# The rows of the first attention's input moved from 1536 to 1088 bytes apart, and the weight buffers from byte 64 to byte 192 of 512

## The chip, the cores and the metric

The kernel runs on one core of a Trainium2 chip. The time is device time in microseconds of one whole execution, from first to last instruction and what lies around them. The engines are named as in the profile: PE is the matrix engine (PEld its weight load), DVE the vector engine, ACT the scalar engine, POOL GpSimd, SP the queue that starts most transfers.

## The reference, cut to what matters

Two transformer blocks over 256 tokens (and 16 meta tokens) of width 1024, all in float32. The first block is this, where `swa` is a windowed attention with sinks and `diff` a differential attention:

```python
u = rms_norm(h, pre_mix_gain[l])
qa, ka, va, qb, kb, vb, g = jnp.split(u @ w_in[l], SPLITS, axis=-1)
...
merged = g_swa * (o_swa @ w_branch_swa[l]) + g_diff * (o_diff @ w_branch_diff[l])
h = h + rms_norm(merged @ w_out[l], post_mix_gain[l])
u = rms_norm(h, pre_ffn_gain[l])
gate_up = u @ w_ffn_in[l]
f = (jax.nn.silu(gate_up[..., :D_FF]) * gate_up[..., D_FF:]) @ w_ffn_out[l]
h = h + rms_norm(f, post_ffn_gain[l])
```

The second block has a gated delta rule beside a sparse attention, then a cross-attention over 256 memory tokens, then a second feed-forward part of the same size (its inner width is 2816 in both), and a last norm.

## The kernel before

**How a product is made.** Activations lie transposed: 128 partitions by 8 rows (`k`), each row the 256 tokens of 128 channels (272 with the meta tokens). A float32 operand is split into two parts of the reduced type `float32r`: `split` writes the rounded part `h` with ACT (L288, L291) and the rest `l` with DVE (L289, L292). `gemm` (L325) makes one block of 128 output channels from 24 matmuls: for each of 8 rows the weight slice `wh` with the input's `h` and `l`, then for each of 8 rows `wl` with `h`. Each matmul loads its own 128x128 weight slice, which is 512 bytes in a partition, and streams one input row of 256 columns (1024 bytes) or 272 columns (1088 bytes). The load for the next matmul runs while the present one streams, so at any time PE reads one input row and one weight slice. `load_w` makes `wh` (ACT, L309) and `wl` (DVE, L311) from `raw`, a transfer of 512 KB that SP starts; all three have their own buffers of 4096 bytes in a partition.

**Which stages there are.** First attention (14 to about 250 us in the profile): 16 queries and 16 gates (32 `gemm` of 256 columns), 8 value blocks of the differential and 2 of the windowed attention (10 `gemm` of 272 columns), the keys as plain float32 matmuls from `u` (L341), and, woven in between, scores (L539), transposes (L597, L606) and weighted sums (L619, L621). Then branch and output products, the first feed-forward part (`ffn_in`: 44 blocks, then 528 matmuls on `f_h` and `f_l`), the memory's keys and values (L821 to L823), the second block's mixer, the cross-attention, the second feed-forward part (44 blocks), and at the end 330 matmuls on L1650 to L1654 with the roles turned: there the weights `wh`, `wl` stream (512 or 256 columns) and the slices of `f_h`, `f_l` are loaded.

**Where things lie.** What counts here is the place of a buffer within 512 bytes of a partition. Every weight slice begins at byte 64 of 512. The input rows of the stages begin at byte 128 of 512: `AT` holds for each of them an offset in elements that brings them there, in tiles a little larger than the rows. For the first attention `AT["first"]` is 112 and the rows are `3 * P` elements (1536 bytes) apart, so that all eight begin at byte 128; its tiles take 12,736 bytes, and `ul` begins 16 elements further in its tile, which undoes the other remainder of that size. The later `uh`, `ul` of the first feed-forward part come out of the same pool, and there the rows are 1024 bytes apart. `mem_h` and `mem_l` begin at byte 64, as the weights do. In what follows the distance of a matmul is the first byte of the row that it streams, less the first byte of the weight slice that is loaded meanwhile, within 512. It is 64 in the first attention's 42 `gemm`s (768 matmuls of 256 columns and 240 of 272) and in 3600 matmuls behind it (128 `gemm`s of 24, and the 528 on `f_h` and `f_l`), 0 in the memory's 384 matmuls, and 448 (that is, 64 bytes below) in the last 330.

**What sets the order.** The code's order is a proposal: a scheduler with a time model of its own places the instructions on each engine and reuses memory by it, and `tc.keep_in_program_order` pins a few. Where a tile lies and which earlier tile it follows there is therefore part of the schedule. In each feed-forward part three blocks have one more matmul, which adds a product with a slice of zeros (`zero`, L328) after the fourth.

Of the kernel before, what the change touches and what calls it, by code (L numbers as in the profile page):

```python
# [17 lines left out]
F32R = mybir.dt.float32r  # L18
# [7 lines left out]
P = 128  # L26
NT = 256
NM = 16
NK = NT + NM
NP = NT + 32  # L30
D = 1024
KT = D // P
# [181 lines left out]
AT = {'ffn1': 112, 'xatt': 0, 'ffn2': 112, 'mem_h': 112, 'mem_l': 112, 'mix_h': 0, 'mix_l': 0, 'ox_h': 0, 'ox_l': 0, 'f': 0, 'first': 112}  # L214
# [7 lines left out]
def _program(tc, d, out):  # L222
# [4 lines left out]
    def new_pool(stack, name, bufs=1, space=None, side=None):  # L227
        kw = {} if space is None else {"space": space}
        if side is not None:
            kw["side"] = side  # L230
        return stack.enter_context(tc.tile_pool(name=name, bufs=bufs, **kw))

    with ctx:
# [4 lines left out]
        gpool = new_pool(ctx, "gen")  # L238
# [3 lines left out]
        hT = rpool.tile([P, KT, NK], F32, name="hT", tag="resA")  # L242
# [14 lines left out]
        def G(n, j=0):  # L257
            o, w = _GC[n]
            return gcol[:, o + j:o + j + 1]
# [25 lines left out]
        def split(h, l, src, gain=None):  # L285

            if gain is None:
                m = act.activation(h, src, AF.Copy)  # L288
                dve.tensor_tensor(l, src, h.bitcast(F32), OP.subtract)  # L289
            else:  # L290
                m = act.activation(h, src, AF.Copy, scale=gain)  # L291
                dve.scalar_tensor_tensor(l, src, gain, h.bitcast(F32), OP.mult, OP.subtract)  # L292
            return m
# [50 lines left out]
        def gemm_long(src, xs, n, use):  # L344

            ps = None
            for k in range(0, len(xs), KT):
                part = xs[k:k + KT]
                ps = gemm(src[:, k * P:(k + len(part)) * P], part, n, use, first=(k == 0),
                          last=(k + KT >= len(xs)), ps=ps)  # L350

        def rsqrt_of(psum_pool, acc, ones, n, out_t):

            st = psum_pool.tile([P, 512], F32, name="st", tag="o")
            pe.matmul(st[:, :n], ones, acc, start=True, stop=True)
            rsqrt_chain(st[:, :n], n, out_t)
# [42 lines left out]
        def sumsq(k, src, acc, n):  # L399
            if k == 0:  # L400
                act.activation(acc, src, AF.Square)
            else:
                s = gpool.tile([P, NK], F32, name="sq", tag="sq", bufs=2)
                act.activation(s[:, :n], src, AF.Square)
                dve.tensor_tensor(acc, acc, s[:, :n], OP.add)
# [4 lines left out]
        def new_u():  # L410
            uh = gpool.tile([P, KT, NK], F32R, name="uh", tag="uh")
            ul = gpool.tile([P, KT, NK], F32R, name="ul", tag="ul")
            return uh, ul

        def rows_at(t, at):

            return t[:, at:at + KT * NT].rearrange("p (a b) -> p a b", a=KT)

        def new_u_at(at, at_l):
            return [rows_at(gpool.tile([P, KT * NK], F32R, name="u" + e, tag="u" + e), a)  # L420
                    for e, a in (("h", at), ("l", at_l))]

        def parts_at(pool_, name, at_h, at_l):
            return [rows_at(pool_.tile([P, KT * NT + P], F32R, name=name + e), at)
# [10 lines left out]
        apool = new_pool(apx, "a")  # L435

        u = gpool.tile([P, KT, NK], F32, name="u", tag="u")
        uh, ul = ([t[:, at + k * 3 * P:at + k * 3 * P + NK] for k in range(KT)] for t, at in (
            (gpool.tile([P, KT * 3 * P + 112], F32R, name="u" + e, tag="u" + e), AT["first"] + (0, 16)[e == "l"])
            for e in "hl"))  # L440

        st = opool.tile([P, 512], F32, name="st", tag="o")
        for _ in range(WARM):
# [21 lines left out]
        rs = gpool.tile([P, NK], F32, name="rs", tag="rs", bufs=2)  # L465
        rsqrt_chain(st[:, :NK], NK, rs)
        for k in range(KT):
            split(uh[k], ul[k], u[:, k, :])
        us = [(uh[k][:, :NT], ul[k][:, :NT]) for k in range(KT)]
        us_v = [(uh[k], ul[k]) for k in range(KT)]  # L470
        us_k = [u[:, k, :] for k in range(KT)]
        ist.close()

# [31 lines left out]
        at = ExitStack()  # L505
# [264 lines left out]
        first = [None]  # L770
# [80 lines left out]
        rsm = mhp.tile([P, NT], F32, name="rsm")  # L851
        act.activation(rsm, st[:, :NT], AF.Copy)

        def post_norm(src_w, xs, gain, res, res_out, g_next, at=0, at_l=0, whole=False):

            fg = mpool.tile([P, 8, NT], F32, name="fg", tag="fg")
            acc = gpool.tile([P, NK], F32, name="acc", tag="acc", bufs=1)[:, :NT]
            for j in range(8):
                def use(o, j=j):
                    act.activation(fg[:, j, :], o, AF.Copy, scale=G(gain, j))  # L860
                    sumsq(j, o, acc, NT)
                gemm_long(src_w[j], xs, NT, use)
            rr = gpool.tile([P, NK], F32, name="rs", tag="rs", bufs=2)
            rsqrt_of(opool, acc, ones_d, NT, rr[:, :NT])
            if whole:
                u = gpool.tile([P, KT, NK], F32, name="u", tag="uh")
            else:
                uh, ul = new_u_at(at, at_l)
            acc2 = gpool.tile([P, NK], F32, name="acc2", tag="acc2", bufs=1)[:, :NT]
            for j in range(8):  # L870
                dve.tensor_tensor(fg[:, j, :], fg[:, j, :], rr[:, :NT], OP.mult)  # L871
                pool.tensor_tensor(res_out[:, j, :], fg[:, j, :], res[:, j, :NT], OP.add)
                if whole:
                    act.activation(u[:, j, :NT], res_out[:, j, :], AF.Copy, scale=G(g_next, j))
                else:
                    split(uh[:, j, :NT], ul[:, j, :NT], res_out[:, j, :], G(g_next, j))
                sumsq(j, res_out[:, j, :], acc2, NT)
            rs2 = gpool.tile([P, NK], F32, name="rs", tag="rs", bufs=2)
            rsqrt_of(opool, acc2, ones_d, NT, rs2[:, :NT])
            if whole:  # L880
                return [u[:, k, :NT] for k in range(8)], rs2[:, :NT]
            return [(uh[:, k, :NT], ul[:, k, :NT]) for k in range(8)], rs2[:, :NT]

        h1 = rpool.tile([P, KT, NT], F32, name="h1", tag="resB")
        us, rs = post_norm(d["w_out1"], [(m_h[:, k, :], m_l[:, k, :]) for k in range(8)],
                           "post_mix", hT, h1, "pre_ffn", at=AT["ffn1"], at_l=AT["ffn1"] + 16)

        def ffn_in(pool_, src_w, us, rs, f_h, f_l):
            zeros = pool_.tile([96, P], F32R, name="zeros")
            pool.memset(zeros.bitcast(F32), 0.0)  # L890
            for j in range(FT):
# [7 lines left out]
                def use_u(o, sg=sg, j=j):  # L899
# [42 lines left out]

        x1 = rpool.tile([P, KT, NK], F32, name="x1", tag="resA")[:, :, :NT]
        us, rs = post_norm(d["w_fo1"], [(f_h[:, k, :], f_l[:, k, :]) for k in range(FT)],
                           "post_ffn", h1, x1, "g_mix", whole=True)
        fst.close()
# [500 lines left out]
        t = tpool.tile([P, 512], F32, name="t", tag="t")  # L1447
# [26 lines left out]
        t = tpool.tile([P, 512], F32, name="t", tag="t")  # L1474
# [62 lines left out]
        added = []  # L1537

        def residual(src_w, xs, res, res_out, g_next, late=(), more=0, at=0):
            uh, ul = new_u_at(at, at)  # L1540
            acc = gpool.tile([P, NK], F32, name="acc", tag="acc", bufs=1)[:, :NT]
            for j in range(8):
                def use(o, j=j):
                    dve.tensor_tensor(res_out[:, j, :], o, res[:, j, :], OP.add)
                    added.append(split(uh[:, j, :NT], ul[:, j, :NT], res_out[:, j, :], G(g_next, j)))
                    sumsq(j, res_out[:, j, :], acc, NT)
                ps = ppool.tile([P, 512], F32, name="s", tag="s") if 2 <= j < 2 + more else None
                gemm(src_w[j], xs, NT, use, ps=ps, late=late if j < 2 + more else ())
            rs2 = gpool.tile([P, NK], F32, name="rs", tag="rs", bufs=2)
            rsqrt_of(opool, acc, ones_d, NT, rs2[:, :NT])  # L1550
            return [(uh[:, k, :NT], ul[:, k, :NT]) for k in range(8)], rs2[:, :NT]

        x2 = rpool.tile([P, KT, NT], F32, name="x2", tag="resB")
        us, rs = residual(d["w_out2"], [(mix_h[:, k, :], mix_l[:, k, :]) for k in range(8)], x1, x2, "g_xattn", (0,1,2,3), 2, AT["xatt"])
        b2.close()

# [23 lines left out]
        for h in range(4):  # L1580
# [4 lines left out]
            t = tpool.tile([P, 512], F32, name="t", tag="t")  # L1585
            t3 = t.rearrange("p (a b) -> p a b", a=2)
            for qb in range(2):
# [9 lines left out]
                l = xpool.tile([P, 1], F32, name="l1", tag="l1", bufs=4)  # L1597
# [19 lines left out]
            split(ox_h[:, 2 * h:2 * h + 2, :], ox_l[:, 2 * h:2 * h + 2, :], o)  # L1617
        x3 = rpool.tile([P, KT, NK], F32, name="x3", tag="resA")[:, :, :NT]
        us, rs = residual(d["w_xo"], [(ox_h[:, k, :], ox_l[:, k, :]) for k in range(8)], x2, x3, "g_ffn", (4,5,6,7), 2, AT["ffn2"])
        xa.close()  # L1620
        mst.close()
# [8 lines left out]
        for qb in range(2):  # L1630
            for kk_ in range(2):
                t = tpool.tile([P, 512], F32, name="t", tag="t")
# [36 lines left out]
        for qb in range(2):  # L1669
# [13 lines left out]
            a = mpool.tile([P, 1], F32, name="ra", tag="ra", bufs=2)  # L1683
# [32 lines left out]
```

## Time and profile before

| | us |
|---|---|
| median of 3 runs | 1007.73 (1005.29 to 1007.76) |
| the profiled execution, whole | 1007.77 |
| its span, first to last instruction | 1005.9 |
| PE busy in the span | 982.8 |
| DVE, ACT, POOL busy | 685.1, 541.3, 222.8 |

The span leaves out 1.9 us around it. A busy engine is one with an instruction under way; PE's matmuls overlap, so a busy PE may still be slower than it could be, and the measure of its pace is the time from one matmul's start to the next one's. The views used are the page's head, the table by stretches, the chain of work that ended last, and PE's timeline.

### The profile page before, as it was taken

Reading aid. Unit: us, or ns where it says so; the run is one execution under the profiler, and the core shown is the slowest. Engines: PE = TensorE matmul, PEld = TensorE weight load, DVE = VectorE, ACT = ScalarE, POOL = GpSimd, SP = SyncE. Lnnn points to the kernel's source line nnn. Section 1 sums busy time; section 2 is a strip of 40 time slices with the busy share of each in tenths; the row PEclk is TensorE's granted clock in tenths of the full one; section 3 lists DMA queues with packets and bytes.
Section 4 is the critical chain, followed back from the end, with each engine's and each line's share of the span. In section 5 each row is a group of like instructions: output and inputs, shape, how many; then the busy total and the mean of one; then the engine's idle time right before and its main releaser. Section 6 shows DMA issues by size and latency. Waiting matters only on the chain.

```text
span 1005.9 us, 18620 instructions
## 1 busy us (share of the span) xinstructions
PE 982.8 (98%) x7218; PEld 915.2 (91%) x7218; DVE 685.1 (68%) x1466; ACT 541.3 (54%) x1097; POOL 222.8 (22%) x258
## 2 busy tenths in 40 slices
PE   9999999999999999999999899999999999999996
PEld 8888898998988989999999888787799999999885
DVE  6788789788655776656544739967687686566534
ACT  5566657667545755555544444335676554444433
POOL 5534326233230213121100312121021011212002
PEclk9999999999999999999999999999999999999999
DMA  6433333332435465555666232333056155555651
GB/s 238 151 110 104 123 126 106 106 126 87 165 120 194 148 210 199 186 184 187 211 199 195 85 127 84 126 105 105 1 167 203 70 181 185 185 186 189 208 189 64
DMA packets 42023, 149.26 MB, mean 148 GB/s; under 512 B 4728, under 2 KB 5376, under 8 KB 41808
## 3 DMA queue, kind: packets, MB, share of 16 engines
q1 hardware_dynamic: 40896, 145.47, 43.8%
q0 software_dynamic: 608, 2.03, 0.7%
q8 instruction: 56, 0.92, 0.4%
q10 hardware_dynamic: 432, 0.59, 0.2%
q14 instruction: 31, 0.25, 0.1%
HBM read 147.01 MB, written 1.06 MB: 147 GB/s over the span
## 4 chain that ended last, share of the span: by engine, by line
PE 57%; DVE 9%; ACT 2%; issue 1%; ACTq 0%; DVEq 0%
PE mm L325 36%; PE mm L341 4%; PE s L325 2%; PE ac L1653 2%; PE ac L1654 2%; PE ac L1650 2%; DVE wl L311 1%; DVE fg L871 1%; PE mm L1413 1%; PE mm L823 1%; DVE ul L292 1%; PE mm L821 1%; PE mm L822 1%; DVE y L1014 1%; DVE base L1158 0%
## 5 line engine op out<-in xcount | busy, mean ns | idle before, releaser
L311 DVE TENSOR_TENSOR wl<-raw,wh 128x1024 fp32r<-128x1024 f32 (+1 forms) x232 | 285.0, 1229 | 101.1 <-ACT wh L309 94.3
L309 ACT ACTIVATE wh<-raw 128x1024 fp32r<-128x1024 f32 (+1 forms) x232 | 242.8, 1048 | 175.0 <-PE mm L325 100.9
L325 PE MATMUL mm<-uh,wh 128*128 128x256 f32 (+1 forms) x1040 | 257.6, 284 | 0.0
L325 PE MATMUL mm<-ul,wh 128*128 128x256 f32 (+1 forms) x1040 | 255.8, 282 | 0.4 <-DVE ul L292 0.4
L325 PEld LDWEIGHTS mm<-uh,wh 128*128 128x128 f32 x1040 | 195.3, 188 | 2.8 <-ACT wh L309 0.6
L325 PEld LDWEIGHTS mm<-ul,wh 128*128 128x128 f32 x1040 | 195.3, 188 | 1.2 <-DVE ul L292 0.8
L325 PE MATMUL mm<-uh,wl 128*128 128x256 f32 (+1 forms) x1040 | 152.2, 283 | 0.0
L325 PEld LDWEIGHTS mm<-uh,wl 128*128 128x128 f32 x1040 | 134.6, 188 | 0.8
L341 PE MATMUL mm<-u,raw 128*128 128x256 f32 (+1 forms) x464 | 109.3, 386 | 0.0
L897 POOL TENSOR_TENSOR sg<-sg,rs 128x256 f32<-128x256 f32 x44 | 50.7, 1154 | 232.1 <-ACT sg L896 232.1
L341 PEld LDWEIGHTS mm<-u,raw 128*128 128x128 f32 x464 | 85.5, 190 | 14.0 <-issue 0.9
L901 DVE TENSOR_TENSOR ft<-mm,sg 128x256 f32<-128x256 f32 x42 | 17.8, 424 | 50.8 <-PE mm L325 49.6
L325 PE MATMUL mm<-f_h,wh 128*128 128x256 f32 x176 | 42.5, 279 | 0.0
L325 PE MATMUL mm<-f_l,wh 128*128 128x256 f32 x176 | 42.5, 279 | 0.0
L895 DVE TENSOR_TENSOR sg<-mm,rs 128x256 f32<-128x256 f32 x40 | 16.9, 423 | 32.2 <-PE mm L325 32.2
L288 ACT ACTIVATE f_h<-ft 128x256 fp32r<-128x256 f32 x44 | 18.3, 417 | 38.1 <-DVE ft L901 38.1
L1653 PE MATMUL ac<-wh,f_l 128*128 128x512 f32 (+1 forms) x110 | 38.3, 349 | 0.0
L1650 PE MATMUL ac<-wh,f_h 128*128 128x512 f32 (+1 forms) x110 | 38.3, 348 | 0.0
L1654 PE MATMUL ac<-wl,f_h 128*128 128x512 f32 (+1 forms) x110 | 38.0, 349 | 0.0
L896 ACT ACTIVATE sg<-sg 128x256 f32<-128x256 f32 x44 | 18.1, 417 | 33.4 <-DVE sg L895 33.4
L325 PEld LDWEIGHTS mm<-f_l,wh 128*128 128x128 f32 x176 | 33.0, 188 | 0.0
L325 PEld LDWEIGHTS mm<-f_h,wh 128*128 128x128 f32 x176 | 33.0, 188 | 0.0
(545 smaller groups left out, 2104.7 us busy)
## 6 DMA issues: line engine op xcount, KB each, us to landing
raw<-w_gu SPq DMA_DIRECT2D x88, 512.0 KB, 4.1
raw<-w_dn SPq DMA_DIRECT2D x22, 512.0 KB, 4.3
raw<-w_pr SPq DMA_DIRECT2D x20, 512.0 KB, 3.4
raw<-w_gate SPq DMA_DIRECT2D x16, 512.0 KB, 3.5
raw<-w_out SPq DMA_DIRECT2D x16, 512.0 KB, 3.6
raw<-w_fo SPq DMA_DIRECT2D x16, 512.0 KB, 3.5
raw<-w_kb SPq DMA_DIRECT2D x8, 512.0 KB, 3.5
raw<-w_vb SPq DMA_DIRECT2D x8, 512.0 KB, 3.5
```

Source lines behind the costliest of these rows:

```text
L288: m = act.activation(h, src, AF.Copy)
L309: act.activation(h[:, :kt * c], raw[:, :kt * c], AF.Copy)
L311: eng.tensor_tensor(l[:, :kt * c], raw[:, :kt * c], h[:, :kt * c].bitcast(F32), OP.subtract)
L325: pe.matmul(o, w[:, k * P:(k + 1) * P], xs[k][i], start=(first and n_ == 0), stop=(last and n_ == len(steps) - 1))
L341: pe.matmul(o, raw[:, k * P:(k + 1) * P], x, start=(k == 0), stop=(k == len(xs) - 1))
L895: dve.tensor_tensor(sg, o, rs, OP.mult)
L896: act.activation(sg, sg, AF.Silu)
L897: pool.tensor_tensor(sg, sg, rs, OP.mult)
L901: dve.tensor_tensor(t, o, sg, OP.mult)
L1650: m = pe.matmul(o, f_h[:, k, tok], h[:, cols], start=(k == 0), stop=False)
L1653: pe.matmul(o, f_l[:, k, tok], h[:, cols], start=False, stop=False)
L1654: pe.matmul(o, f_h[:, k, tok], l[:, cols], start=False, stop=(k == FT - 1))
```

## The change

The first attention's `uh` and `ul` become plain tiles of 8 rows of 272 elements. Their rows are 1088 bytes apart, so each begins 64 bytes further within 512 than the one before. The two tiles take 8704 bytes each in place of 12,736, so what is allocated above them comes down by 8064 bytes: the buffers `raw`, `wh`, `wl`, and the memory's tiles, now begin at byte 192 of 512. The tiles below stay where they were, and the first feed-forward part's rows still begin at byte 128.

```diff
-        def new_u_at(at, at_l):
-            return [rows_at(gpool.tile([P, KT * NK], F32R, name="u" + e, tag="u" + e), a)
-                    for e, a in (("h", at), ("l", at_l))]
+        def new_u_at(at):
+            return [rows_at(gpool.tile([P, KT * NK], F32R, name="u" + e, tag="u" + e), at) for e in "hl"]
...
-        uh, ul = ([t[:, at + k * 3 * P:at + k * 3 * P + NK] for k in range(KT)] for t, at in (
-            (gpool.tile([P, KT * 3 * P + 112], F32R, name="u" + e, tag="u" + e), AT["first"] + (0, 16)[e == "l"])
-            for e in "hl"))
+        uh, ul = new_u()
...
-            split(uh[k], ul[k], u[:, k, :])
-        us = [(uh[k][:, :NT], ul[k][:, :NT]) for k in range(KT)]
-        us_v = [(uh[k], ul[k]) for k in range(KT)]
+            split(uh[:, k, :], ul[:, k, :], u[:, k, :])
+        us = [(uh[:, k, :NT], ul[:, k, :NT]) for k in range(KT)]
+        us_v = [(uh[:, k, :], ul[:, k, :]) for k in range(KT)]
...
-                           "post_mix", hT, h1, "pre_ffn", at=AT["ffn1"], at_l=AT["ffn1"] + 16)
+                           "post_mix", hT, h1, "pre_ffn", at=AT["ffn1"])
```

`new_u` (L410) makes two tiles `[P, KT, NK]`. After the change the distances are these: in the first attention 0, 64, 128 and so on up to 448 for the rows 0 to 7; 448 for the 3600 matmuls that had 64; 0 for the memory's, as before; 64 for the last 330, which had 448. The slice of zeros lies at distance 384 in the first feed-forward part in both, and at 384 in place of 0 in the second.

No instruction is added or removed, and the order of transfers on SP is the same. The smaller tiles change which buffers follow which in memory, and the scheduler then places some instructions of the first attention otherwise, from about 92 to 200 us of the profile; all later order is the same. (After the change the line numbers from L437 on are 3 less.)

On PE, at about 91.3 us, where the scores of two heads (`kb_h`, `kb_l` against `qh`, `ql`) meet a value block of 272 columns (`uh`, `wl`); before:

```order
L539 MATMUL s<-kb_l,qh 128x272
L539 MATMUL s<-kb_h,qh 128x272
L539 MATMUL s<-kb_h,ql 128x272
L539 MATMUL s<-kb_l,qh 128x272
L325 MATMUL mm<-uh,wl 128x272 x3
L597 MATMUL t<-base,pr_222 32x128
L539 MATMUL s<-kb_h,qh 128x272
L539 MATMUL s<-kb_h,ql 128x272
L539 MATMUL s<-kb_l,qh 128x272
L325 MATMUL mm<-uh,wl 128x272 x2
```

and with the change:

```order
L536 MATMUL s<-kb_l,qh 128x272
L536 MATMUL s<-kb_h,qh 128x272
L536 MATMUL s<-kb_h,ql 128x272
L536 MATMUL s<-kb_l,qh 128x272
L536 MATMUL s<-kb_h,qh 128x272
L536 MATMUL s<-kb_h,ql 128x272
L536 MATMUL s<-kb_l,qh 128x272
L325 MATMUL mm<-uh,wl 128x272 x5
L594 MATMUL t<-base,pr_222 32x128
```

Three scores have moved up to the other four, and the value block's matmuls stand together behind them. Over the whole first attention the 192 score matmuls stand in 56 separate groups before and in 52 with the change.

On POOL, in the middle of the first attention, where the rotation of a query (`ropem`, `rot`, `qraw`) and the norm of a finished head (`ms`, `rr`, `osb`) take turns; before:

```order
L514 TENSOR_TENSOR ropem<-rawq,cqt 128x256
L657 TENSOR_TENSOR ms<-ms,rr 128x256
L515 TENSOR_TENSOR rot<-rot,sqt 128x256
L658 TENSOR_TENSOR ms<-ms,rr 128x256
L516 TENSOR_TENSOR qraw<-ropem,rot 128x256
L659 TENSOR_SCALAR ms<-ms 128x256
L660 TENSOR_TENSOR rr<-rr,ms 128x256
L661 TENSOR_TENSOR osb<-osb,rr 128x256
```

and with the change:

```order
L511 TENSOR_TENSOR ropem<-rawq,cqt 128x256
L512 TENSOR_TENSOR rot<-rot,sqt 128x256
L654 TENSOR_TENSOR ms<-ms,rr 128x256
L513 TENSOR_TENSOR qraw<-ropem,rot 128x256
L655 TENSOR_TENSOR ms<-ms,rr 128x256
L656 TENSOR_SCALAR ms<-ms 128x256
L511 TENSOR_TENSOR ropem<-rawq,cqt 128x256
L657 TENSOR_TENSOR rr<-rr,ms 128x256
```

The query's rotation now goes ahead of the norm's first step, and the next query's first step ahead of the norm's last two.

## Rows read from the trace of the kernel before

**Rows 1.** The page's head: span, and busy time of each engine.
```profile
span 1005.9 us, 18620 instructions
PE 982.8 (98%) x7218; PEld 915.2 (91%) x7218; DVE 685.1 (68%) x1466; ACT 541.3 (54%) x1097; POOL 222.8 (22%) x258
```

**Rows 2.** Stretches: length, then busy us (count) by engine, granted clock, DMA share, GB/s.
```profile
170.00:250.00 80.00, 80.00 (x612) 73.13 (x609) 65.80 (x159) 52.74 (x133) 21.30 (x28) 1.00 0.32 106
401.00:486.00 85.00, 85.00 (x724) 85.00 (x723) 51.88 (x75) 44.45 (x61) 17.77 (x16) 1.00 0.56 185
...
823.00:938.00 115.00, 115.00 (x972) 114.72 (x971) 71.51 (x105) 57.81 (x86) 25.32 (x22) 1.00 0.58 188
```

**Rows 3.** Chain that ended last, 401 to 486 us: start, length, work.
```profile
430.16 55.95 PE mm L325 x475
```

**Rows 4.** PE's timeline in the memory's keys: start, length, instruction.
```profile
344.84 0.28 PE L325 MATMUL mm<-mem_h,wh 128*128 128x256 f32 x1
...
345.92 0.28 PE L325 MATMUL mm<-mem_l,wh 128*128 128x256 f32 x1
```

**Rows 5.** PE's timeline in the second block's output product, distance 64.
```profile
734.29 0.28 PE L325 MATMUL s<-mix_h,wh 128*128 128x256 f32 x1
...
747.89 0.28 PE L325 MATMUL mm<-uh,wh 128*128 128x256 f32 x1
```

**Rows 6.** PE's timeline around the first product with zeros, distance 64.
```profile
376.72 0.28 PE L325 MATMUL mm<-uh,wh 128*128 128x256 f32 x1
...
378.65 0.28 PE L325 MATMUL mm<-ul,wh 128*128 128x256 f32 x1
378.77 0.28 PE L328 MATMUL mm<-ul,zeros 96*128 96x256 f32 x1
...
379.94 0.28 PE L325 MATMUL mm<-ul,wh 128*128 128x256 f32 x1
```

**Rows 7.** PE's timeline in the last 330 matmuls, distance 448.
```profile
944.34 0.28 PE L1654 MATMUL ac<-wl,f_h 128*128 128x256 f32 x1
...
944.79 0.39 PE L1650 MATMUL ac<-wh,f_h 128*128 128x512 f32 x1
...
946.88 0.28 PE L1650 MATMUL ac<-wh,f_h 128*128 128x256 f32 x1
...
947.59 0.39 PE L1650 MATMUL ac<-wh,f_h 128*128 128x512 f32 x1
```

**Rows 8.** PE's timeline where distances differ: cross-attention (128), first attention (0, 448 in turn).
```profile
783.64 0.28 PE L1614 MATMUL o<-ptx_h,vx_h 128*128 128x256 f32 x1
...
785.06 0.28 PE L325 MATMUL mm<-ox_l,wh 128*128 128x256 f32 x1
...
100.40 0.28 PE L619 MATMUL o<-pl,va_h 128*128 128x256 f32 x1
...
100.87 0.28 PE L621 MATMUL o<-pm,vam 96*128 96x256 f32 x1
```

**Rows 9.** PE's timeline in a value block of 272 columns, distance 64.
```profile
47.50 0.29 PE L325 MATMUL mm<-uh,wh 128*128 128x272 f32 x1
...
48.76 0.29 PE L325 MATMUL mm<-uh,wh 128*128 128x272 f32 x1
```

**Rows 10.** PE's timeline at the scores of the first order fence.
```profile
91.33 0.29 PE L539 MATMUL s<-kb_h,ql 64*128 64x272 f32 x1
91.46 0.28 PE L539 MATMUL s<-kb_l,qh 64*128 64x272 f32 x1
91.67 0.65 PE L325 MATMUL mm<-uh,wl 128*128 128x272 f32 x3
...
92.35 0.40 PE L539 MATMUL s<-kb_h,qh 64*128 64x272 f32 x1
92.59 0.28 PE L539 MATMUL s<-kb_h,ql 64*128 64x272 f32 x1
```

**Rows 11.** Groups, 14 to 250 us: count, busy us, mean ns, idle before and its releaser.
```profile
L657 POOL TENSOR_TENSOR ms<-ms,rr 128x256 f32<-128x256 f32 x8 | 7.4, 920 | 34.0 <-ACT rr L656 34.0
```

More of the change, by code (lines that the diff above doesn't have):

```diff
@@ L852, in _program, with post_norm @@
         act.activation(rsm, st[:, :NT], AF.Copy)
-        def post_norm(src_w, xs, gain, res, res_out, g_next, at=0, at_l=0, whole=False):
+        def post_norm(src_w, xs, gain, res, res_out, g_next, at=0, whole=False):
             fg = mpool.tile([P, 8, NT], F32, name="fg", tag="fg")
@@ L867, in post_norm @@
             else:
-                uh, ul = new_u_at(at, at_l)
+                uh, ul = new_u_at(at)
             acc2 = gpool.tile([P, NK], F32, name="acc2", tag="acc2", bufs=1)[:, :NT]
@@ L1539, in residual @@
         def residual(src_w, xs, res, res_out, g_next, late=(), more=0, at=0):
-            uh, ul = new_u_at(at, at)
+            uh, ul = new_u_at(at)
             acc = gpool.tile([P, NK], F32, name="acc", tag="acc", bufs=1)[:, :NT]
```

## The prediction

> **What bounds the kernel now.** I read the page's head first: PE is busy in 982.8 of 1005.9 us, the next engine in 685 [rows 1]. [...]
>
> The pace is not one number. [...] The long chain of the first feed-forward part has 475 matmuls in 55.95 us, 117.8 ns each [rows 3]. The memory's keys take 9 steps from 344.84 to 345.92: 120 ns [rows 4]. The output product of the second block takes 120 steps from 734.29 to 747.89: 113.3 ns [rows 5]. Same shape, same clock, no wait of an engine among them. The stages differ in where the streamed row and the weight slice lie: distance 0 in rows 4, distance 64 in rows 3 and 5. So at 64 there are two paces, 118 and 113, and at 0 there is a third, 120. Which of the two paces a run at 64 has is a matter of how it was entered: the first feed-forward part starts at 113 (17 steps from 376.72 to 378.65, 113.5), and from its first product with zeros, whose own distance is 384, it goes at 118 (10 steps from 378.77 to 379.94, 117) and stays there to the end [rows 6, 3]. A run keeps its pace until something disturbs it.
>
> **The change, part by part.** The sum is made against the profiled execution, 1007.77 whole, which is the median's 1007.73 to four hundredths.
>
> *The first attention's rows.* 768 matmuls of 256 columns and 240 of 272 leave distance 64 for distances that go up by 64 from row to row. The trace has no such sequence in a `gemm`. The nearest rows are products whose distance is other than 64 or changes: the cross-attention's weighted sums at 128 take 12 steps in 1.42 us, 118.3 ns, and the first attention's own weighted sums at 0 and 448 by turns take 4 steps in 0.47 us, 117.5 ns [rows 8]. I take 118.0 against the 117.8 that most of these `gemm`s have now: 1008 x 0.2 ns = +0.2 us. The bounds are the fastest and slowest steady paces anywhere: 768 x (113.3 - 117.8) = -3.5 us and 768 x (120 - 117.8) = +1.7 us. For 272 columns there is one pace to read, 10 steps in 1.26 us, 126 ns [rows 9]; I leave it, with +-3 ns by the same spread: +-0.7 us.
>
> *The other 3600 matmuls* go from 64 to 448, from 64 bytes ahead of the weights to 64 behind. Here the trace does show the new distance: the last 330 matmuls have it. Their runs of 256 columns go at one pace or the other by turns, 4 steps from 944.34 to 944.79 at 112.5 ns, 6 steps from 946.88 to 947.59 at 118 ns [rows 7]. These are the two paces of distance 64, and none of 120. So I take the pace of the long runs as it is, 117.8, and the term as 0. But a run of six says little of one of a thousand, and the term is large: at 113.3 throughout it would be 3600 x -4.5 = -16 us, at 120 throughout 3600 x 2.2 = +8 us. Those are its bounds.
>
> *What goes at 113 now* is 120 steps of rows 5, some 20 of rows 6 and a few dozen after rows 5, say 200. Entered anew at another distance, I let half of them fall to 118: 100 x 4.5 ns = +0.5 us; bounds 0 and +0.9.
>
> *The last 330* go from 448 to 64. Both paces are seen at both distances; 0, with +-330 x 2 ns = +-0.7 us.
>
> *The memory's 384* stay at distance 0, since rows and weights move together: 0.
>
> *The order in the first attention.* A score that stands alone costs more at its ends than inside: from 91.33 to 91.46 it is 0.13 us, but the last of a group takes from 91.46 to 91.67, 0.21, and the first of one from 92.35 to 92.59, 0.24 [rows 10]. One group less saves 0.08 + 0.11 = 0.19 us; there are 56 groups before and 52 after, so -0.8 us. On POOL the rotation of a query now goes ahead of a head's norm. POOL stands idle 34.0 us before the norm's first step, waiting for ACT [rows 11], and PE has no idle time in this stage [rows 2]; what is moved lies in that slack: 0. If the cover were gone, because buffers now follow each other more closely and a matmul waits for one, a POOL step is 0.9 us [rows 11]; I allow three of them, +-2.7 us, for what a new order may lose or win.
>
> *What is released.* PE being the bound, a faster pace would be followed by the weights: in the feed-forward parts DVE, the next engine, is busy 52 of 85 us [rows 2], and could stand 113 ns (82 of 85) without being late.
>
> The sum: 0.2 + 0 + 0.5 + 0 + 0 - 0.8 = -0.1 us. 1007.77 - 0.1 = **1007.7 us**.
>
> [...] The paces of rows 3 and 4 differ by 2.2 ns with nothing but the distance different that I can see. [...]
>
> **The rivals.**
>
> *Faster: the long runs go at 113.* At 448 half of the runs in rows 7 have that pace, while of the two long runs at 64 in rows 3 and 5 only the shorter has it; and the products with zeros are disturbances in which a run may change its pace, at distances that the change alters. In the first feed-forward part with its second product, 1056 + 528 matmuls, it would be 1584 x 4.5 = -7 us; in the second, 1056 x 4.5 = -4.8 us. One of them gives 1001 to 1003, both 996. Against it: at 64 the disturbances led to 118, and a run at 118 was not seen to speed up. Chance 0.27.
>
> *Slower: the long runs go at 120.* Streaming 64 bytes behind the weights may not be the mirror of streaming 64 ahead, and rows 7 are too short to see a slow drift into the state of rows 4. The place is the two feed-forward parts with the 528, 2640 matmuls; the price is 2640 x 2.2 = 5.8 us, or 8 with all 3600: 1013.5 to 1015.7. It decides once the pace there passes 119 ns (2640 x 1.2 = 3.2 us). For it: distance 0, only 64 bytes away, has this state and keeps it. Against it: no run at 448 shows it. Chance 0.14.
>
> *Slower: the first attention's spread rows.* No row shows distances from 192 to 320 in sequence, and each change of distance is a disturbance. At 122 ns, the 1008 matmuls would be 4 us late: 1012. Chance 0.11, and 0.06 more that the new order brings waits of about that size: 1011.
>
> *The place does nothing.* What differs between rows 3, 4 and 5 may be something else in those stages. Then only the order is left, -0.8: 1007. Chance 0.08, within the forecast's.
>
> **How the numbers follow.** About 0.3%, 3 us, is what a measurement of this kernel can tell from no change. The forecast (1004.7 to 1010.7) has 0.42 with the last rival in it. Faster by more than that is 0.27, from the first rival; slower is 0.14 + 0.11 + 0.06 = 0.31. The range reaches down to one and a half of the fast runs' gains, -10.7 us, 997, and up to the slower feed-forward parts and a little of the order, +6.3, 1014; a tenth is left out at each end. The likeliest case's own range is 1004.7 to 1010.7.
>
> **What would show it.** In the changed kernel's timeline: the pace of the long chain after the last product with zeros in either feed-forward part, 117.8 by the forecast, 113.3 or 120 by the rivals; steps of about 118 in the first attention's gates; 120 in the memory's keys; the score groups' ends as in rows 10 but fewer; PE busy 80 of 80 us in 170 to 250. If the feed-forward parts take other than 85.0 and 115.0 us, the forecast is wrong by that much, and the second term is the one that failed; if the first attention ends more than 3 us from where it does now, it is the first or the last.

## The result, and the profile after

The changed kernel takes **991.3 us** (990.05 to 992.7, four executions) against 1007.75 (1005.29 to 1008.94, four): a ratio of 0.984, with a 95% interval of 0.9818 to 0.9863. The forecast was no change, 1007.7, with a range of 997 to 1014. It was wrong: the time fell by 16 us, out of the range. The rival "the long runs go at 113" is what happened. The ratios below are against executions of the kernel before on the same chip, whose median was 1007.0 to 1007.8.

The page's head after answers to [rows 1]: PE's busy time is 15.6 us less, with as many instructions.

```profile
span 988.8 us, 18641 instructions
...
PE 967.2 (98%) x7218; PEld 902.1 (91%) x7218; DVE 686.8 (69%) x1466; ACT 545.3 (55%) x1097; POOL 223.4 (23%) x258
```

Where the 17.1 us of the span went is read from PE's timeline, from the first matmul of a stage to the first of the next (differences are of the unrounded times):

| stage | before, us | after, us | difference |
|---|---|---|---|
| first attention, from 13.6 | 234.7 | 232.7 | -2.0 |
| branch products | 57.8 | 57.5 | -0.3 |
| output product (m) | 26.9 | 25.9 | -0.9 |
| memory's keys | 20.6 | 20.6 | 0.0 |
| first feed-forward part, 44 blocks | 132.6 | 126.8 | **-5.8** |
| its 528 on f_h and f_l, then the second block's mixer | 233.8 | 231.4 | **-2.4** |
| second block's output product (mix) | 28.1 | 28.8 | +0.8 |
| into the cross-attention | 31.8 | 30.9 | -0.9 |
| product on ox | 27.5 | 27.3 | -0.2 |
| second feed-forward part, 44 blocks | 129.3 | 125.2 | **-4.1** |
| last 330 matmuls and the output | 69.5 | 68.2 | -1.3 |

Not all of the -5.8 is pace. In the profiled execution before, the granted clock stood at 0.5 for 3.4 us of that stage, after PE had waited 1.4 us for `ul`; 15 matmuls there took 213 ns a step, which cost 15 x (213 - 118) = 1.4 us. The profiled execution of the changed kernel had the same wait and a clock of 1.00 in that stage. Columns as in [rows 2], before:

```profile
357.60:361.00 3.40, 3.40 (x19) 3.40 (x18) 3.40 (x8) 0.42 (x1) 0.00 (x0) 0.51 0.91 306
```

Two stretches serve for every kernel below, since in all of them they lie inside the long runs of one feed-forward part each: 430.5 to 475.5 us in the first, 881.5 to 919.5 in the second. Columns as in [rows 2]; PE's count is what is read. Some 2.4 of it began before the stretch (a matmul is under way for 0.28 us), so 385 in 45 us is a pace of 117.6 ns, 399 is 113.5, 382 is 118.5, and in 38 us 325 is 117.8, 338 is 113.2, 323 is 118.5. Of the kernel before:

```profile
430.50:475.50 45.00, 45.00 (x385) 45.00 (x384) 27.41 (x41) 23.31 (x33) 9.11 (x8) 1.00 0.56 184
881.50:919.50 38.00, 38.00 (x325) 38.00 (x324) 22.67 (x34) 18.18 (x27) 8.42 (x7) 1.00 0.57 182
```

and of the changed one:

```profile
430.50:475.50 45.00, 45.00 (x399) 45.00 (x399) 28.60 (x42) 24.83 (x34) 9.09 (x8) 1.00 0.59 191
881.50:919.50 38.00, 38.00 (x338) 38.00 (x337) 24.15 (x36) 20.78 (x28) 7.58 (x8) 1.00 0.58 194
```

Same shape, same granted clock, PE without a gap in both, so the time there is the number of matmuls by their pace, and only the pace is another.

How it came to that pace stands in the chain that ended last, second feed-forward part of the changed kernel (start, length, work), which answers to [rows 3]:

```profile
805.24 3.30 PE s L325 x28
808.54 8.95 PE mm L325 x76
817.49 0.12 PE mm L328
817.61 16.34 PE mm L325 x144
833.96 0.12 PE mm L328
834.08 32.66 PE mm L325 x288
866.74 0.12 PE mm L328
866.87 53.97 PE mm L325 x476
```

The first 104 steps go at 117.8 ns (3.30 / 28, 8.95 / 76). Then comes the first product with zeros (L328), and behind it 144 steps take 16.34 us, 113.5 ns, and so to the end (53.97 / 476 = 113.4). It is [rows 6] turned round: there the first product with zeros led from 113.3 to 117.8.

In the first feed-forward part another product stands some 28 matmuls ahead of the first one with zeros: `s<-cc,base` (L935, L932 in the changed kernel), with weights of 32 x 8, two matmuls. The pace changes there too. Before, the 45 steps ahead of it go at 117.6 ns (5.29 / 45), and the 27 from 375.70 to the first product with zeros at 378.77 [rows 6] at 113.7:

```profile
369.52 5.29 PE mm L325 x45
...
375.70 0.28 PE L325 MATMUL mm<-ul,wh 128*128 128x256 f32 x1
```

In the changed kernel the steps ahead go at 113.8 (5.12 / 45), and the 27 from 370.50 to 373.68 at 117.8:

```profile
364.48 5.12 PE mm L325 x45
...
370.50 0.29 PE L325 MATMUL mm<-ul,wh 128*128 128x256 f32 x1
...
373.68 0.28 PE L328 MATMUL mm<-ul,zeros 96*128 96x256 f32 x1
```

So the changed kernel needed its first product with zeros in both parts, to come back to 113.4. That product is at distance 384 in the first part of both kernels; it led down in the one and up in the other, so its own distance does not say which way.

The memory's keys, whose distance stayed 0, stayed at 120 ns, 7 steps from 336.80 to 337.64, as in [rows 4]:

```profile
336.80 0.28 PE L325 MATMUL mm<-mem_h,wh 128*128 128x256 f32 x1
...
337.64 0.28 PE L325 MATMUL mm<-mem_l,wh 128*128 128x256 f32 x1
```

### The profile page after: what moved, and what is told of

The parts are those of the page before. It is cut to its first block, busy times and chain, and to the rows that moved or that the text cites. A ratio compares the mean times of both kernels' runs of the same rounds, so it can differ in the third digit from the quotient of the medians.

```text
span 988.8 us, 18641 instructions
## 1 busy us (share of the span) xinstructions
PE 967.2 (98%) x7218; PEld 902.1 (91%) x7218; DVE 686.8 (69%) x1466; ACT 545.3 (55%) x1097; POOL 223.4 (23%) x258
## 4 chain that ended last, share of the span: by engine, by line
PE 56%; DVE 8%; ACT 2%; issue 1%; DMA 0%; ACTq 0%; DVEq 0%
PE mm L325 36%; PE mm L341 4%; PE s L325 2%; PE ac L1651 2%; PE ac L1650 2%; PE ac L1647 2%; DVE fg L868 1%; DVE wl L311 1%; PE mm L1410 1%; PE mm L820 1%; PE mm L818 1%; PE mm L819 1%; DVE ul L292 1%; DVE y L1011 1%; DMA raw<-w_xq 0%
## 5 line engine op out<-in xcount | busy, mean ns | idle before, releaser
L325 PE MATMUL mm<-uh,wh 128*128 128x256 f32 (+1 forms) x1040 | 253.1, 282 | 0.0
L325 PE MATMUL mm<-ul,wh 128*128 128x256 f32 (+1 forms) x1040 | 251.2, 281 | 0.2 <-DVE ul L292 0.2
L325 PE MATMUL mm<-uh,wl 128*128 128x256 f32 (+1 forms) x1040 | 148.6, 281 | 0.0
L325 PEld LDWEIGHTS mm<-uh,wl 128*128 128x128 f32 x1040 | 131.9, 188 | 0.5 <-issue 0.2
L511 POOL TENSOR_TENSOR ropem<-rawq,cqt 128x256 f32<-128x256 f32 x16 | 18.4, 1152 | 59.9 <-ACT rawq L508 59.8
L341 PE MATMUL mm<-os,raw 128*128 128x256 f32 x128 | 28.2, 380 | 0.0
```

The source lines that it names most:

```text
L325: pe.matmul(o, w[:, k * P:(k + 1) * P], xs[k][i], start=(first and n_ == 0), stop=(last and n_ == len(steps) - 1))
L341: pe.matmul(o, raw[:, k * P:(k + 1) * P], x, start=(k == 0), stop=(k == len(xs) - 1))
L511: pool.tensor_tensor(m[:, :n], raw[:, :n], c, OP.mult)
```

## The experiments

Theory: the distance sets which paces a run can have, and a product with zeros lets it change between them. Rivals: the first attention's new rows or order; the weights' own place.

### The distance alone

Kernel before, rows moved and nothing else; tiles and the order of every engine stay.

```diff
-AT = {'ffn1': 112, 'xatt': 0, 'ffn2': 112, ... 'mix_h': 0, 'mix_l': 0, 'ox_h': 0, 'ox_l': 0, 'f': 0, 'first': 112}
+AT = {'ffn1': 80, 'xatt': 96, 'ffn2': 80, ... 'mix_h': 96, 'mix_l': 96, 'ox_h': 96, 'ox_l': 96, 'f': 0, 'first': 80}
```

> The kernel before with the input rows of nine stages 128 bytes lower and nothing else different: weights at byte 64 as before, rows at byte 0, so distance 448 for the first attention's 1008 matmuls, both feed-forward input parts (2112) and the products on mix and ox and into the cross-attention (576). The first attention's rows stay 1536 bytes apart, and the order of every engine is that of before. The 528 matmuls on f_h and f_l and the 384 on od and m stay at distance 64. Theory (the distance sets the pace): the 2112 + 576 go at about 114.3 ns as in the changed kernel in place of 117.8, 2688 x 3.5 = -9.4 us, and the first attention's 768 x 3.5 = -2.7 us: about 996, the feed-forward stretches at 113 to 114 ns. Rival (it was the new rows or the new order of the first attention): 1007 to 1008, pace 117.8 throughout. Second rival (it is the weights' own place, not the distance): 1007 to 1008 too, but then the run with the rows moved up stays at 991.

Measured: 993.25 us, ratio 0.9868 (0.9832 to 0.9905). Both stretches have the changed kernel's counts, to one:

```profile
430.50:475.50 45.00, 45.00 (x400) 45.00 (x399) 29.08 (x42) 24.39 (x34) 9.47 (x9) 1.00 0.61 194
881.50:919.50 38.00, 38.00 (x338) 38.00 (x337) 24.05 (x36) 19.30 (x28) 8.35 (x7) 1.00 0.62 194
```

So 14 of the 16 us come with the first attention's old layout, the old order and the weights at their old place: the first rival falls, and the second. No product with zeros lifted this kernel: both parts had come to 113.4 ahead of their first one, the first part behind L935 (from 117.8), the second for the 76 steps before it. The first attention's 660 intervals go at 115.8 in place of 117.6, the 272 columns at 123.8 in place of 126.1. The 528 on f_h and f_l, left at 64, went at 117.8 here although the run came to them at 113.3.

The other way round: the changed kernel with rows moved up by as much.

```diff
-AT = {'ffn1': 112, 'xatt': 0, 'ffn2': 112, ... 'mix_h': 0, 'mix_l': 0, 'ox_h': 0, 'ox_l': 0, ...}
+AT = {'ffn1': 16, 'xatt': 32, 'ffn2': 16, ... 'mix_h': 32, 'mix_l': 32, 'ox_h': 32, 'ox_l': 32, ...}
```

> The changed kernel with the input rows of the feed-forward parts, the cross-attention and the products on mix and ox 128 bytes higher: weights at 192 as in the change, rows at 256, so distance 64 again for 2688 matmuls; the first attention as in the change, the same order on every engine. Theory (distance): these go back to 117.8 ns, 2688 x 3.5 = +9.4 us over the change's 991.3: about 1001. Rival (rows or order of the first attention, or the weights' own place): 991.

Measured: 1004.73 us, ratio 0.9978 (0.9962 to 0.9995), 13.4 above the change.

```profile
430.50:475.50 45.00, 45.00 (x384) 45.00 (x384) 27.38 (x40) 23.61 (x32) 9.12 (x8) 1.00 0.61 187
881.50:919.50 38.00, 38.00 (x325) 38.00 (x325) 23.50 (x34) 19.82 (x28) 8.10 (x7) 1.00 0.60 189
```

Back at 117.8. The loss is 4 us above the theory's. Of these 528 x 4.4 = 2.3 us are the 528 on f_h and f_l: still at 448, they kept the 117.8 with which the run came to them, with no product with zeros among them to lift it. What is left of the gain on the kernel before is 2.5 us. In the profiled executions the first attention is 0.5 us shorter than before and the last 330 with the output 0.8; the rest is not placed, since shorter stages differ by up to 2.7 us one way and 2.0 the other.

### The products with zeros

The same edit in the changed kernel and in the one before:

```diff
-                gemm(src_w[2 * j], us, NT, use_g, ps=bank(0), zero=zeros if j in (3, 6, 12) else None)
+                gemm(src_w[2 * j], us, NT, use_g, ps=bank(0), zero=None)
```

> The changed kernel without the six products with a slice of zeros (three in each feed-forward part), which add nothing to the result. In the changed kernel the second feed-forward part goes at 117.8 for 102 steps up to the first of them, and at 113.3 behind it. Theory (a product with zeros is what lets a run change its pace): without them that part stays at 117.8 to its end, 950 x 4.5 = +4.3 us, and the first part, which came to 113.3 before its first one, stays there: 995 to 996. Rival (at this distance a run comes to 113.3 by itself in the end): 990 to 991, six products less.

> The changed kernel without products with zeros once more, letter for letter the third run's. Its executions gave four times 997.7 to 998.3 and, in the profiled one, 1003.9 with the first feed-forward part at 117.8 for 1469 steps. Theory (at this distance both paces hold, and without products with zeros the entry decides for the whole run): a profiled execution near 998 shows the first part at 113.3, 1469 x 4.4 = 6.5 us less, and the second at 117.8 as in the other; one near 1004 shows 117.8 in both. Rival (the 6 us are something else, a wait elsewhere): a profiled execution near 998 shows 117.8 in the first part all the same.

Measured: 998.2 us (five executions, 997.73 to 1003.89), ratio 0.9913; the second time 999.63 (four, 996.83 to 1002.93), ratio 0.9923. The two profiled executions, 1003.89 and 1000.39, both show 117.8 to the end in both parts; the second:

```profile
430.50:475.50 45.00, 45.00 (x385) 45.00 (x384) 27.36 (x41) 23.66 (x32) 9.10 (x8) 1.00 0.59 186
881.50:919.50 38.00, 38.00 (x325) 38.00 (x325) 22.80 (x34) 20.12 (x28) 8.49 (x7) 1.00 0.58 184
```

Six products less, and 9.3 us more than the profiled 991.08 of the changed kernel: at 448 a run does not come to 113.3 by itself in 1465 steps, and the rival falls. Half of the first expectation fell too: it took the changed kernel's first part to be at 113.3 ahead of its first product with zeros, but behind L932 it is at 117.8 there, as the lines above show, and here it stayed so. And the second test did not show what it was made for: the 3.5 us between its two profiled executions are not the first part's pace. They lie in several places, of which one is the output product, where the granted clock was 0.83 in one and 1.00 in the other; just before, PE had waited 1.6 us for `m_h` and `m_l` in the one and 1.8 in the other. The stretch from 311 to 321 us, columns as in [rows 2], in the execution of 1003.89:

```profile
311.00:321.00 10.00, 9.21 (x65) 9.21 (x66) 5.08 (x7) 5.74 (x10) 0.00 (x0) 0.83 0.63 199
```

and in the one of 1000.39, with 85 matmuls for 65:

```profile
311.00:321.00 10.00, 9.72 (x85) 9.72 (x86) 6.13 (x8) 6.78 (x13) 0.00 (x0) 1.00 0.71 216
```

What pace the executions near 997 had is not known.

> The kernel before without the six products with zeros, distance 64 everywhere. There the first feed-forward part began at 113.3 and went over to 117.8 at the first of them. Theory (the product with zeros is the kick, at this distance to the slow side): the first part stays at 113.3 for its 1584 matmuls, 1480 x 4.5 = -6.7 us: 1001; the second, which began at 117.8, stays as it is. Rival (at distance 64 the pace falls back to 117.8 whatever disturbs it): 1007.

Measured: 999.35 us, ratio 0.9917 (0.9891 to 0.9943).

```profile
430.50:475.50 45.00, 45.00 (x399) 45.00 (x399) 29.06 (x43) 24.18 (x34) 9.12 (x8) 1.00 0.64 195
881.50:919.50 38.00, 38.00 (x325) 38.00 (x324) 22.77 (x34) 20.30 (x27) 7.60 (x7) 1.00 0.59 181
```

As the theory has it: at distance 64 too a run can keep 113.3, here for 1462 steps with the 528 on f_h and f_l in it, if nothing throws it out. The second part, which began at 117.8, kept that. In the kernel before, the products with zeros alone cost 8 us, most of it by the pace behind the first of them (some 1440 steps x 4.4 ns = 6.3 us).

Then the products were moved: `j in (10, 14, 18)` in the changed kernel.

> The changed kernel with the three products with zeros of each feed-forward part moved from the blocks 3, 6 and 12 to 10, 14 and 18 of 22. Theory (at 448 such a product lifts a run from 117.8 to 113.3 and nothing else does): the second part goes at 117.8 up to block 10 in place of 3, 336 matmuls later, 336 x 4.4 = +1.5 us, and turns there; the first likewise if it begins at 117.8, another +1.5: 992 to 995. Rival (a run comes to 113.3 by itself after some hundred matmuls): the turn stays near step 100, and the time at 991.

Measured: 994.38 us (992.66 to 994.76), ratio 0.9866. The chain in its second part:

```profile
806.70 3.30 PE s L325 x28
809.99 48.53 PE mm L325 x412
858.52 0.12 PE mm L328
858.64 21.78 PE mm L325 x192
880.42 0.12 PE mm L328
880.55 21.78 PE mm L325 x192
```

Now 440 steps go at 117.8 (48.53 / 412), 336 more than the 104 of the changed kernel, and the turn to 113.4 (21.78 / 192) stands again at the first product with zeros. The first part turned in the same way. This is the plainest proof that the product is what lifts the run there.

The products on all 128 rows, `zeros` made `[P, P]` in the changed kernel:

> The changed kernel with the six products with zeros on all 128 rows in place of 96; the same order on every engine. Theory (one more matmul, which makes the sequence of h and l rows start anew, is what lets the pace change): as the changed kernel, 991, and the second feed-forward part goes from 117.8 to 113.3 at the first of them. Rival (the 96 rows are what does it, a slice of another shape between full ones): as without them, 117.8 to the end in the second part, 996 to 998.

Measured: 997.46 us, ratio 0.9904 (0.9883 to 0.9925), undecided: the second part turned at the first of them, so 96 rows are not needed, but the first part did not turn at any of three. That is one of four from 117.8, against five of six on 96 rows at this distance (runs below included).

```profile
430.50:475.50 45.00, 45.00 (x385) 45.00 (x384) 27.56 (x40) 23.45 (x33) 9.10 (x8) 1.00 0.59 188
881.50:919.50 38.00, 38.00 (x338) 38.00 (x336) 24.23 (x35) 20.68 (x29) 8.00 (x7) 1.00 0.59 194
```

### All eight distances

Kernel before, with `AT` set so that each stage has another distance; tiles and order stay. The three settings are those of the three runs below, in their order.

```diff
+AT = {'ffn1': 0, 'xatt': 48, 'ffn2': 16, ... 'mix_h': 48, 'mix_l': 48, 'ox_h': 48, 'ox_l': 48, 'f': 0, 'first': 96}
...
+AT = {'ffn1': 48, 'xatt': 112, 'ffn2': 64, ... 'mix_h': 112, 'mix_l': 112, 'ox_h': 112, 'ox_l': 112, 'f': 0, 'first': 32}
...
+AT = {'ffn1': 16, 'xatt': 96, 'ffn2': 48, ... 'mix_h': 96, 'mix_l': 96, 'ox_h': 96, 'ox_l': 96, 'f': 0, 'first': 0}
```

> The kernel before with nothing moved but the input rows, by stage: first attention at distance 0, first feed-forward part at 128, second at 192, the 576 products into the cross-attention and on mix and ox at 256; the 528 on f_h and f_l and the 384 on od and m stay at 64. Theory (448, rows just below the weights, is the one place from which the products with zeros lead to 113.3): 117.8 in both feed-forward parts, 120 in the first attention, 768 x 2.2 = +1.7 us: 1008 to 1009. Rival (64 is the one bad place, and 0; any other one is as good as 448): both feed-forward parts at 113.3 behind their first product with zeros, some 950 x 4.5 = -4.3 us each, and the 576 at 113.3, -2.6 us, so 998.

Measured: 1005.4 us, ratio 0.9979 (0.9966 to 0.9993). First part at 128, second at 192, and 15 us of the product on mix at 256:

```profile
430.50:475.50 45.00, 45.00 (x382) 45.00 (x381) 27.20 (x39) 23.34 (x32) 9.07 (x8) 1.00 0.57 183
881.50:919.50 38.00, 38.00 (x338) 38.00 (x337) 23.91 (x36) 19.31 (x28) 8.41 (x7) 1.00 0.60 194
...
734.00:749.00 15.00, 15.00 (x127) 15.00 (x126) 14.02 (x20) 10.92 (x21) 6.33 (x4) 1.00 0.49 157
```

> As the run before it with the places that are left: first attention at distance 256, first feed-forward part at 320, second at 384, the 576 at 0. Theory (448 alone): 117.8 in both feed-forward parts, 120 in the 576, +1.3 us: 1008 to 1009. Rival (only 0 and 64 are bad): both parts at 113.3, -8.6 us, the first attention faster by up to 768 x 2 = -1.5 us, so 998.

Measured: 1008.97 us, ratio 1.0025 (1.0012 to 1.0039). First part at 320, second at 384:

```profile
430.50:475.50 45.00, 45.00 (x385) 45.00 (x384) 27.75 (x40) 23.42 (x33) 9.12 (x8) 1.00 0.59 188
881.50:919.50 38.00, 38.00 (x323) 38.00 (x322) 22.51 (x33) 18.11 (x27) 8.38 (x7) 1.00 0.56 181
```

Theory and rival both fell in the pair. 192 went as fast as 448, against the one; 128, 256, 320 and 384 are not, against the other. 256 behaves as 0 (120 ns: 15 us / 124.6), 320 as 64 (first part: 113.3 for 25 steps, 117.8 from the first product with zeros on), 384 as 128 (steps of 115 to 122 in a pattern of five, 288 of them in 34.17 us: mean 118.7; at 128 the 382 in 45 us are 118.5). That made a new theory, the distance within 256, and a run to test it with the parts exchanged:

> The kernel before with the input rows moved by stage: first attention at distance 128, first feed-forward part at 192, second at 320, the 576 at 448; the 528 and the 384 stay at 64. New theory (what counts is the distance within 256: 0 gives 120 ns, 128 a mixture of 118.7, 64 and 192 have both 113.3 and 117.8, and a product with zeros leads to 117.8 at 64 and to 113.3 at 192): the first part ends at 113.3, also behind a start at 117.8; the second at 117.8, also behind a start at 113.3; the first attention near 118.7. First part 1056 x -4.4 = -4.6 us, the 576 up to -2.5, the first attention +0.7: 1001 to 1004 against 1007. Rival (each part of the model has its own pace, whatever the distance; before, 192 was seen in the second part alone and 320 in the first alone): the first part at 117.8, the second at 113.3.

Measured: 1001.62 us, ratio 0.9945 (0.9928 to 0.9962), inside the theory's 1001 to 1004.

```profile
430.50:475.50 45.00, 45.00 (x399) 45.00 (x398) 29.11 (x42) 24.15 (x33) 9.76 (x9) 1.00 0.61 197
881.50:919.50 38.00, 38.00 (x325) 38.00 (x325) 23.88 (x35) 18.95 (x28) 7.84 (x7) 1.00 0.62 192
```

192 in the first part: 113.5; 320 in the second: 117.8; the first attention at 128: 118.9. The rival falls. At 192 and in this run at 320 the long runs had these paces ahead of their first product with zeros, so a lift was seen at 448 alone, and a fall at 64 and 320.

### Two versions meant to be faster

The kernel before with 128 bytes more in the first `ul` tile, the keys' rows brought to 448, and one product with zeros more in each feed-forward part (left out here: `mem_l`, as `mem_h`, and two offsets that keep the later rows at byte 128):

```diff
-            (gpool.tile([P, KT * 3 * P + 112], F32R, name="u" + e, tag="u" + e), AT["first"] + (0, 16)[e == "l"])
+            (gpool.tile([P, KT * 3 * P + 112 + (0, 32)[e == "l"]], F32R, name="u" + e, tag="u" + e), (96, 112)[e == "l"])
...
-        mem_h = mhp.tile([P, 8, NT], F32R, name="mem_h")
+        mem_h = mhp.tile([P, 8 * NT + P], F32R, name="mem_h")[:, 112:112 + 8 * NT].rearrange("p (a b) -> p a b", a=8)
...
-zero=zeros if j in (3, 6, 12) else None
+zero=zeros if j in (0, 3, 6, 12) else None
```

> The first attention's rows 1536 bytes apart as before, its ul tile 128 bytes longer so that weights lie at byte 192 as in the change, rows at 128: distance 448 in the first attention, both feed-forward parts, on od, m, mix, ox, f, and, with 448 bytes ahead in its tiles, in the memory's keys too; the order of before but for one product with zeros more, in the first block of each feed-forward part. Theory (distance and kick): from the change's 991.3, first attention 768 x -2.4 = -1.8 and 240 x -1.7 = -0.4 us (paces as in the run with the rows moved back), the keys 192 x -6 = -1.2, the second part's first 100 steps -0.4, one product each +0.2: 987 to 988. Rival (short runs take either pace by chance): no better than the change, 990 to 992.

Measured: 992.42 us, ratio 0.9858 (0.9842 to 0.9874): no better than the change. The keys did go at 113.5 behind their first 37 steps and the first attention at 116.4, but that stage still took 1.4 us longer than in the change (234.1 against 232.7), 172 steps of the output product and the keys' first went at 117.8, and the first part stayed there for 170 until its third product with zeros.

So more of them were put in, in the first blocks of each stage (`ZS` is their slice; the branch and output products are left out here):

```diff
+            gemm(d["w_xk"][j], mems, NT, ..., zero=ZS if j in (0, 1) else None)
+            gemm(src_w[j], xs, NT, use, ps=ps, ..., zero=ZS if j in (1, 2, 4) else None)
...
+            zeros = ZS
...
+zero=zeros if j in (1, 2, 3, 6, 12) else None
```

> The kernel with distance 448 everywhere, with more products with zeros: one in the first blocks of the branch product, the output product, the memory's keys, the second block's output product, the cross-attention's output, and five in each feed-forward part (blocks 1, 2, 3, 6, 12). Theory: each of these stages turns to 113.3 early. From that kernel's 992.4: its first part 170 x -4.4 = -0.7 us, the output product 170 x -4.4 = -0.7, branch 45 x -4.4 = -0.2, cross-attention's output 70 x -4.4 = -0.3, some 12 products more +1.4: 991.5 or less, 990 where all of them turn. Rival (short runs do not turn, the products are only a cost): 993.8.

Measured: 995.7 us, ratio 0.9883 (0.9865 to 0.99), 3.3 slower. The output product and the keys went at 113.4, and so did the product on mix, which had that pace without added products too; the product on ox stayed at 117.8. The waits of PE from 330 to 376 us (us in total, times, longest) say what became of it:

```profile
PE s L327 <- ACT wh L311: 3.7, 2, 3.1
PE mm L327 <- DVE wl L313: 1.7, 1, 1.7
PE s L327 <- DVE ul L294: 0.2, 1, 0.2
```

In the kernel without the added products PE waited 1.8 us there, for `ul`; 3.8 us went into new waits. The keys bridge the norm between output product and feed-forward part, and the weights came late for a PE that was done sooner. ACT itself waited for a transfer ahead of the `wh` (from 340 to 362 us):

```profile
ACT wh L311 <- DMA raw<-w_gu: 6.9, 2, 4.8
```

What made them late is not shown: the norm needs ACT and DVE as the weights do, but the scheduler also placed some of ACT's and DVE's instructions otherwise in this stage. No kernel tried was faster than the changed one.

## Why the prediction was wrong, and where it was right

**The other 3600 matmuls**, taken as 0: the step that failed. The two parts' inputs and the 528 alone gained 5.8, 4.1 and 2.3 us, 12.2 of the 17.1; less the 1.4 of the granted clock, 10.8. The rival priced just these at 11.8, so mechanism and size were in the text, with the smaller chance. I chose by the last 330 at 448 [rows 7], because both paces stood there, and called them the two paces of distance 64. That they occur at both distances was right; what differs is where a product with zeros leads, and runs of four to six can't show that. From 113.3, at 64 and 320, both products with zeros that met it led to 117.8, and none of 16 led up from there; at 192 and 448 none of 26 led down, and 6 of 10 led up from 117.8. (Counted over the long runs of the kernels above except the last.) The weights' place is not what makes this difference: with weights at byte 64, a product led down from 113.3 at distance 64 and none of six did at 448; with weights at 192, none of six led up at 64 and six of ten did at 448.

Two readings of the trace before were wrong as well. The first feed-forward part does not start at 113: it goes at 117.8 until L935 and at 113.3 only for the steps between L935 and the first product with zeros. And so the sentence that spoke against the rival, "a run at 118 was not seen to speed up", was not true even at 64: this run sped up at L935.

**The first attention's rows**, +0.2: right. At the eight distances in turn 654 intervals have a mean of 118.2, 272 columns 125.5: +0.4 and -0.15 us.

**The order there**, -0.8: right in sign, too small. In the six traces with the change's rows and order there (the change, the rows moved up, the two without products with zeros, the products moved, and those with 128 rows) the stage takes 232.3 to 234.1, mean 233.4, against 234.7 and 234.9 in the two with those of before. That is -1.4, and -1.7 without the paces, with a scatter of 1 us. No run changed the order alone, so that this rest is the order's is not shown.

**What goes at 113**, +0.5: right in sign and inside its bounds; the product on mix fell to 117.8 and took 0.8 us longer.

**The last 330**, 0 with +-0.7: the size was off. The 512 columns go at 228.9 in place of 232.6, 198 x 3.7 = -0.7, the 256 at 113.3 in place of 116.3, 132 x 3.0 = -0.4: -1.1.

**The memory**, 0, and the weights that follow a faster PE in the two parts: right.

## What to carry to other kernels

Where PE is busy throughout, read its pace, the time from one matmul's start to the next one's, stage by stage at the same clock; here 4.4 ns a step in the feed-forward parts made 10.8 of the span's 17.1 us. Then set the streamed rows' place against the weights' place and try it alone, by an offset within a tile: here 128 bytes were worth 14 us. Before a rare product of another shape is left in a long run, see which pace it leads to, and before a bridge between two stages is made faster, see what it bridges.

## What the runs showed of the hardware

| distance within 256 | paces of 256 columns, ns | a product with zeros leads to | read in |
|---|---|---|---|
| 0 (0, 256) | 120, and 120.4 at 256 | not seen | [rows 4]; first run of distances |
| 64 (64, 320) | 113.3 and 117.8 | 117.8 | [rows 3, 5, 6]; second and third run of distances |
| 128 (128, 384) | mean 118.5 and 118.7 | the same | first and second run of distances |
| 192 (192, 448) | 113.3 and 117.8 (117.8 at 448 in long runs alone) | 113.3, or no change | first and third run of distances; the changed kernel and its variants |

All of these at a granted clock of 1.00; no long stretch read here went below 113.2 ns (400 in 45 us, with the rows moved back). A weight load runs beside the matmul ahead of its own, which is why the distance takes the slice that is loaded meanwhile: before, the load for the `uh` matmul that starts at 376.50 us begins at 376.38, with the `ul` matmul, and takes 0.19 us.

Products with zeros are not the only ones at which a run changes. Behind L935, in one profiled execution of each kernel, the run went on at 113.3 in all five kernels with weights at byte 64 and two paces (at distances 64, 64, 448, 320 and 192), where it had come at 117.8, and at 117.8 in all eight with weights at byte 192, where it had come at 113.3 but for the one with the rows moved up. Distance 448 stands in both groups, and so does 64; here the outcome goes with the weights' place, or with something that moves with it, and not with the distance.

What makes the period of 256 bytes, what sets the pace with which a run begins, and why four products of ten did not lift it (three of them those on 128 rows, in one execution) stays open; the trace shows the pace and not its cause.
